# One of the seven products of a gate/up stage done by a second level of Strassen's form, for two feature tiles at a time

## The chip, the cores and the metric

The kernel runs on one core of a Trainium2 chip. The time is device time in microseconds (us). The core has an engine for matmuls (PE, with its weight loads shown apart as PEld), a vector engine (DVE), a scalar engine (ACT), GpSimd (POOL) and SyncE (SP), which here issues nearly all DMAs. Each engine takes its instructions in the order of the program and waits on semaphores for the others.

## The reference, cut to what matters

The program is one step of a hybrid decoder layer on 1048 tokens (16 meta tokens, 1024 of a prompt, 8 samples) of width 1024: a feed-forward block, a mixing stage (HGRN2 and Mamba-2 heads with their projections), a second feed-forward block and a final norm. The change is in the two feed-forward blocks (FFN), each with 2816 hidden features:

```python
def swiglu(x, wg, wu, wd):
    return (jax.nn.silu(x @ wg) * (x @ wu)) @ wd

h = h + 0.5 * swiglu(rmsnorm(h, n1), w1g, w1u, w1d)
...
h = h + 0.5 * swiglu(rmsnorm(h, n2), w2g, w2u, w2d)
```

All is in float32. The second FFN leaves out the 16 meta tokens and has 1032.

## The kernel before, in words

**Precision.** A float32 product is made of three matmuls with operands split into a high and a low part (`mm3`, L160 to L165): high x high, high x low, low x high. The high part of a weight is a cast on ACT, the low part a subtraction on DVE (`Left.hi` L460 and `Left.lo` L464, the records of L462 and L466).

**Gate and up as one Strassen product.** A feature tile is 128 of the 2816 hidden features; there are 22 in each FFN, taken in eleven pairs. For one tile, the left side is a 2 x 2 block matrix: gate and up weights by the two halves of the 1024 input features. The right side is the input, in two halves of the features and two lanes of the tokens. Seven products (Strassen's form with few additions) give gate and up for both lanes: `g0`, `g1`, `u0`, `u1`. Tokens are in four quarters of Q (262 in the first FFN, 258 in the second); a product is made for two halves of the tokens, `c` = 0 and 1, and each of these is four blocks of 128 input features x three matmuls of Q columns: 12 matmuls, one step. A tile has 14 steps in the order of `ORDER` = 1, 6, 2, 5, 7, 3, 4. The operands of the seven products (`Blocks`, L317) lie in SBUF for the whole stage, in 28 of the 30 buffers "u".

**Weights.** `Left` loads the four blocks of a tile (products 1, 7, 4, 2), forms the four others by sums on DVE (L458) and splits all seven. `plan` (L472) says ahead of which step each is issued, counted from the tile's first step: loads at -11 and -10, sums at -7 to -5, the cast of the i-th product at 2i - 4 and its subtraction at 2i - 3. Raw blocks have eight buffers "r", split ones six buffers "ws".

**After a product.** Products 2, 3 and 4 accumulate into the banks of 1, 5 and 7. There are two buffers of two PSUM banks, taken in turns, and four single banks "mis", which this stage uses in its first tile alone. `post` (L549) runs behind the second half's step: after 1 a copy on ACT (L551), after 6, 5, 7, 3 and 4 an addition on DVE (L553, L560, L562, L564, L572), after 2 a multiplication by the norm's factor (`times_r`, L546) and silu on ACT (L558). After 3 follow the factor for `g1` and `u1` and silu (L581), after 4 the factor for `u0` and both hidden products (`product_`, L587).

**Hidden blocks.** `Hidden.jobs` (L629) forms, for each pair of tiles, four differences of hidden blocks on DVE (L647) for the down projection, itself in Strassen's form, and stores all seven operands to DRAM (L650) through SP. They are issued ahead of given steps of the second tile and of the next pair.

**The order** is written out by hand: `Steps` (L416) holds PE's steps, and ahead of each step the functions registered for it; `ffn` (around L810 to L832) fixes the order of PE, DVE, ACT and SP to that of the program. `down` begins where the last pair ends; its loads and splits (L667, L671, L675, L717, L732, L737) are registered for steps before that. In the first FFN, the first tile's rows are late and finished in the second pair's first steps.

Of the kernel before, what the change touches and what calls it, by code (L numbers as in the profile page):

```python
# [9 lines left out]
F32 = mybir.dt.float32  # L10
F32R = mybir.dt.float32r
# [6 lines left out]
P = 128  # L18
# [298 lines left out]
class Blocks:  # L317
# [123 lines left out]
class Left:  # L441
# [80 lines left out]
def halves(t):  # L522
    return t.rearrange("p (c t) -> p c t", c=2)


def pair(K, S, wg, wu, f, ops, spread, hid, late_r, first=None):
# [16 lines left out]

    def times_r(n, i, cs, src=None):
        t = temp(n, cs)
        nc.vector.tensor_mul(t, t if src is None else src, spread.lanes(i, cs))  # L546
        return t

    def post(p, cs, b):  # L549
        if p == 1:  # L550
            nc.scalar.copy(temp("z", cs), b)  # L551
        elif p == 6:
            nc.vector.tensor_add(temp("v", cs), b, temp("z", cs))  # L553
        elif p == 2 and (f == 0 or wait and f == 1):
            nc.scalar.copy(temp("g0", cs), b)
        elif p == 2:
            t = times_r("g0", 0, cs, b)
            nc.scalar.activation(t, t, AF.Silu)  # L558
        elif p == 5:
            nc.vector.tensor_add(temp("x", cs), b, temp("v", cs))  # L560
        elif p == 7:
            nc.vector.tensor_add(temp("u1", cs), b, temp("x", cs))  # L562
        elif p == 3:
            nc.vector.tensor_add(temp("g1", cs), b, temp("v", cs))  # L564
# [5 lines left out]
            times_r("u1", 1, cs)  # L570
        else:
            nc.vector.tensor_add(temp("u0", cs), b, temp("v", cs))  # L572
            if f == 0:
                return
            times_r("u0", 0, cs)
            for n in range(2):
                product_(n, cs)

    def silu(n, cs):
        t = times_r(f"g{n}", n, cs)  # L580
        nc.scalar.activation(t, t, AF.Silu)  # L581

    def product_(n, cs):
        if "h" not in tm:
            tm["h"] = True
            hid.append(K.slot("s", K.T))
        nc.vector.tensor_mul(halves(hid[0][:, n * 2 * K.Q : n * 2 * K.Q + 2 * K.Q])[:, cs], temp(f"g{n}", cs), temp(f"u{n}", cs))  # L587

    if not first:
# [32 lines left out]
class Hidden:  # L622
# [6 lines left out]
    def jobs(self, S, i, hid, e0, e1):  # L629

        K = self.K
        t, b = {}, {}

        def block(n):

            return hid[n // 2][0][:, n % 2 * 2 * self.K.Q : n % 2 * 2 * self.K.Q + 2 * self.K.Q]

        def val(p):
            return b[p] if p in b else block({1: 0, 12: 1, 2: 2, 3: 3}[p])

        def sub(p, x, y):
            s = {5: 0, 6: 0, 7: 1, 4: 1}[p]
            if s not in t:
                t[s] = K.slot("s", self.K.T)
            o = (p in (6, 4)) * 2 * self.K.Q
            b[p] = t[s][:, o : o + 2 * self.K.Q]
            K.nc.vector.tensor_sub(b[p], val(x), val(y))  # L647

        def store(p):
            K.nc.sync.dma_start(self.d[p][:, :, i, :], halves(val(p)))  # L650
# [5 lines left out]
        for at, p in ((e0 + 2, 1), (e1 + 1, 3), (e1 + 2, 2)):  # L656
            S.before(at, lambda p=p: store(p))

    def load(self, S, p, at):
# [147 lines left out]
def ffn(K, wg, wu, wd, ops, spread, src, first, after, late_r):  # L807

    NF = DFF // P
    wgv = wg.rearrange("(k p) c -> p k c", p=P)
    wuv = wu.rearrange("(k p) c -> p k c", p=P)
    wdv = wd.rearrange("(f p) c -> p f c", p=P)
    E = mybir.EngineType

    with K.tc.manual_schedule(engines={E.PE, E.DVE, E.Activation, E.SP}):
        S = Steps()
        S.before(14, lambda: K.banks(2))
        hidden = Hidden(K)  # L820
        for i in range(NF // 2):
            hid, e = [], []
            for f in (2 * i, 2 * i + 1):
                hid.append([])
                pair(K, S, wgv, wuv, f, ops, spread, hid[-1], late_r, first if f == 0 else None)
                e.append(len(S.steps))
            hidden.jobs(S, i, hid, *([late_r + 6, max(late_r + 7, e[1])] if i == 0 else e))
        h = []
        down(K, S, wdv, hidden, src, h, after)
        S.run()  # L830
    return h
# [1252 lines left out]
```

## Time and profile before

| | us |
|---|---|
| median of three runs | 1995.35 |
| lowest and highest of them | 1993.51, 1996.27 |
| span of the profiled execution, first to last instruction | 1985.6 |
| busy in it: PE, its weight loads | 1935.3, 1897.1 |
| busy in it: DVE, ACT, POOL | 1452.2, 834.8, 82.3 |

The profiled execution is one more execution; the page gives its span and no time around it. Busy times overlap, as the engines run beside each other. The gate/up stage of the first FFN ends near 490 us of the span, that of the second runs from about 1300 to 1741 us. In rows of the order of time the columns are: start, duration, engine, line, operation, output <- input, shape, and in brackets how long the engine stood idle before and what ended that.

### The profile page before, as it was taken

The page shows a single profiled execution, that of the slowest core. Times are in us where ns is not written, and L with a number is a line of the kernel's source. Part 1 is how long each engine was busy: PE and PEld are TensorE (multiplying, and loading weights), DVE is VectorE, ACT ScalarE, POOL GpSimd, SP SyncE. Part 2 cuts the span into 40 slices and gives each one's busy share as a digit, 9 for nine tenths or more (in the row PEclk, how much of TensorE's full clock was granted, in tenths as well). Part 3 has the DMA queues.
Part 4 walks back from the last instruction along what each step waited for, and adds up shares of the span by engine and source line. Part 5 has one row for each costly group of instructions (what it writes and reads, how often), then busy time and mean ns, then how long its engine had stood idle before and what let it go on. Part 6 is the DMA issues. An engine that isn't in the chain of part 4 may idle for free.

```text
span 1985.6 us, 40881 instructions
## 1 busy us (share of the span) xinstructions
PE 1935.3 (97%) x16681; PEld 1897.1 (96%) x16681; DVE 1452.2 (73%) x2504; ACT 834.8 (42%) x1591; POOL 82.3 (4%) x135
## 2 busy tenths in 40 slices
PE   7999999999999999999999999999999999999997
PEld 6999999999999999998988989999999999999997
DVE  7777777777688776676655547887777777768973
ACT  7522222224534655465544535742222222344352
POOL 4000000000000310000000001200000000000000
PEclk9999999999999999999999999999999999999999
DMA  6233242324976542222522154224232433587851
GB/s 218 77 100 98 82 129 82 111 83 155 299 242 222 181 126 60 65 91 75 168 78 76 57 168 135 74 81 128 81 112 81 118 92 103 157 243 238 273 178 69
DMA packets 323876, 258.45 MB, mean 130 GB/s; under 512 B 17568, under 2 KB 299424, under 8 KB 323680
## 3 DMA queue, kind: packets, MB, share of 16 engines
q1 hardware_dynamic: 323448, 255.79, 42.0%
q8 instruction: 132, 2.16, 0.4%
q14 instruction: 56, 0.46, 0.1%
q0 software_dynamic: 224, 0.04, 0.0%
q10 hardware_dynamic: 16, 0.00, 0.0%
HBM read 190.79 MB, written 65.05 MB: 129 GB/s over the span
## 4 chain that ended last, share of the span: by engine, by line
PE 77%; DVE 12%; DMA 4%; ACT 4%; issue 2%; SPq 1%; POOL 0%; DVEq 0%; ACTq 0%; POOLq 0%
PE acc L163 24%; PE acc L165 24%; PE acc L164 23%; DVE u L675 1%; DVE u L352 1%; DVE ws L737 1%; DMA r<-in_w_ffn_up_dram 1%; DVE s L761 1%; DMA s<-in_x_prompt_dram 1%; DVE ws L466 1%; DVE u L727 1%; DMA r<-in_w_ffn_down_dram 1%; DMA u<-hd 1%; DVE t L546 1%; ACT ws L732 1%
## 5 line engine op out<-in xcount | busy, mean ns | idle before, releaser
L163 PE MATMUL acc<-u,ws 128*128 128x258 f32 (+4 forms) x4504 | 1314.6, 292 | 8.9 <-DVE t L562 1.9
L165 PE MATMUL acc<-u,ws 128*128 128x258 f32 (+4 forms) x4504 | 1304.8, 290 | 3.5 <-DVE ws L466 3.4
L164 PE MATMUL acc<-u,ws 128*128 128x258 f32 (+4 forms) x4504 | 1304.9, 290 | 3.2 <-DVE u L352 2.6
L163 PEld LDWEIGHTS acc<-u,ws 128*128 128x128 f32 x4504 | 852.3, 189 | 14.8 <-issue 5.3
L164 PEld LDWEIGHTS acc<-u,ws 128*128 128x128 f32 x4504 | 855.5, 190 | 6.2 <-DVE u L352 3.8
L165 PEld LDWEIGHTS acc<-u,ws 128*128 128x128 f32 x4504 | 852.0, 189 | 5.1 <-DVE ws L466 4.6
L466 DVE TENSOR_TENSOR ws<-r,ws 128x512 fp32r<-128x512 f32 x308 | 212.6, 691 | 78.9 <-ACT ws L462 78.9
L462 ACT CAST ws<-r 128x512 fp32r<-128x512 f32 x308 | 173.8, 614 | 5.2 <-DVE r L458 4.6
L581 ACT ACTIVATE t<-t 128x524 f32<-128x524 f32 (+1 forms) x47 | 29.9, 640 | 298.3 <-DVE t L546 298.3
L458 DVE TENSOR_TENSOR r<-r,r 128x512 f32<-128x512 f32 x176 | 121.1, 690 | 9.7 <-DMA r<-in_w_ffn_up_dram 8.0
L558 ACT ACTIVATE t<-t 128x516 f32<-128x516 f32 (+1 forms) x41 | 26.2, 639 | 201.5 <-DVE t L546 201.5
L675 DVE TENSOR_TENSOR u<-u,u 128x1048 fp32r<-128x1048 f32 (+3 forms) x84 | 97.1, 1158 | 10.2 <-ACT u L671 10.2
L546 DVE TENSOR_TENSOR t<-t,u 128x524 f32<-128x524 f32 (+1 forms) x135 | 90.3, 697 | 2.8
L230 POOL TENSOR_TENSOR t<-t,t 128x262 f32<-128x262 f32 (+1 forms) x56 | 54.4, 980 | 830.6 <-ACT t L229 827.4
L158 DVE TENSOR_TENSOR ws<-r,ws 128x512 fp32r<-128x512 f32 x88 | 60.6, 699 | 34.9 <-ACT ws L157 34.5
L732 ACT CAST ws<-u 128x512 fp32r<-128x512 f32 (+1 forms) x72 | 42.2, 586 | 99.8 <-DVE u L727 97.8
L671 ACT CAST u<-u 128x1048 fp32r<-128x1048 f32 (+3 forms) x84 | 82.8, 988 | 1.3 <-DMA u<-hd 1.3
L761 DVE SCALAR_TENSOR_TENSOR s<-acc,s 128x524 f32<-128x524 f32 (+3 forms) x88 | 54.6, 644 | 36.4 <-PE acc L165 36.1
L737 DVE TENSOR_TENSOR ws<-r,ws 128x512 fp32r<-128x512 f32 (+1 forms) x84 | 57.3, 693 | 29.2 <-ACT ws L732 29.2
L732 ACT CAST ws<-r 128x512 fp32r<-128x512 f32 (+1 forms) x84 | 47.5, 582 | 65.2 <-DVE r L727 34.8
L551 ACT COPY t<-acc 128x524 f32<-128x524 f32 (+3 forms) x46 | 26.4, 574 | 103.6 <-PE acc L165 103.6
L157 ACT CAST ws<-r 128x512 fp32r<-128x512 f32 x88 | 53.7, 618 | 32.4 <-PE acc L165 28.5
(386 smaller groups left out, 1833.3 us busy)
## 6 DMA issues: line engine op xcount, KB each, us to landing
r<-in_w_ffn_down_dram SPq DMA_DIRECT2D x128, 256.0 KB
hd<-s SPq DMA_DIRECT2D x93, 258.0 KB
r<-in_w_ffn_gate_dram SPq DMA_DIRECT2D x88, 256.0 KB
r<-in_w_ffn_up_dram SPq DMA_DIRECT2D x88, 256.0 KB
hd<-s SPq DMA_DIRECT2D x77, 262.0 KB
u<-hd SPq DMA_DIRECT2D x36, 516.0 KB
u<-hd SPq DMA_DIRECT2D x28, 524.0 KB
r<-in_w_in_dram SPq DMA_DIRECT2D x56, 256.0 KB
```

Of the source, the lines that this page charges most:

```text
L163: mm(ps, whi, xhi, start=first, stop=False, skip_group_check=more)
L164: mm(ps, whi, xlo, start=False, stop=False, skip_group_check=more)
L165: mm(ps, wlo, xhi, start=False, stop=last, skip_group_check=more)
L458: self.K.nc.vector.tensor_tensor(self.raw[p], self.raw[x], self.raw[y], op)
L462: self.K.nc.scalar.copy(self.w[p][:, : self.n * P], self.raw[p])
L466: self.K.nc.vector.tensor_sub(t[:, 512 : 512 + w], self.raw[p], t[:, :w].bitcast(F32))
L546: nc.vector.tensor_mul(t, t if src is None else src, spread.lanes(i, cs))
L671: K.nc.scalar.copy(hi, lo.bitcast(F32))
L675: K.nc.vector.tensor_sub(lo, lo.bitcast(F32), hi.bitcast(F32))
L732: nc.scalar.copy(w[p, j, g][:, : n * P], src)
L737: nc.vector.tensor_sub(t[:, 512 : 512 + n * P], box[0], t[:, : n * P].bitcast(F32))
L761: nc.vector.scalar_tensor_tensor(t, b, 0.5, t, ALU.mult, ALU.add)
```

## The change

From the third pair of each FFN (the fifth tile) on, a tile makes six of its seven products itself, in the order `ORDER6`. Product 3 of both tiles of the pair is made together: the left side is a 2 x 2 block matrix (two tiles by two halves of the product's 512 input features), the right side the operand of product 3 (the same halves by the two token halves `c`), and seven inner products of two blocks each take the place of two times two halves of four blocks. An inner product is 2 x 3 = 6 matmuls of Q columns. A pair now has 12 steps for tile A, and for tile B ten, two inner ones (products 1 and 6; 5 and 7), the two of product 4, and two inner ones (2 and 3; 4), the last with 6 matmuls. The inner products go into the four "mis" banks.

Their results are added, Q columns at a time, to what the tile holds as `x` (the sums after product 5), so `x` becomes `g1`; what the second tile's bank after 4 gives goes into `v`, which becomes `u0`. The gate multiplication and silu for `g1` and the hidden product of lane 1 of both tiles come after the last inner step, at the next pair's first four steps, and the differences and their stores later than before. The raw weights of product 3 are kept unsplit until tile B, where four sums, four casts and four subtractions make the inner left operands. The right operands (three new ones, one written in place) are made once in each FFN, during the second pair and the first tile of the third.

```diff
-    def plan(self, S, s0, late, sums):
+    def plan(self, S, s0, late, sums, order=ORDER, last=0):
+        n = len(order)
+        his = [2 * i - 4 + late + last * (i == n - 1) for i in range(n)]
...
-            (ORDER, [2 * i - 4 + late for i in range(7)], self.hi),
-            (ORDER, [2 * i - 3 + late for i in range(7)], self.lo),
+            (order, his, self.hi),
+            (order, [d + 1 for d in his], self.lo),
...
+ORDER6 = (1, 6, 2, 5, 7, 4)
+class Inner:
+    def operands(self):
...
+        return [
+            lambda: whole(a, 1, 0), lambda: whole(b, 0, 0), lambda: sub(b, a, b), lambda: cast(5, b), lambda: low(5, b),
+            lambda: whole(d, 1, 1), lambda: sub(b, d, b), lambda: cast(6, b), lambda: low(6, b),
+            lambda: sub(a, d, a), lambda: cast(7, a), lambda: low(7, a),
+            lambda: whole(d, 0, 1), lambda: sub(b, d, b),
+        ], [lambda: cast(4, b), lambda: low(4, b)]
...
+        for at, fn, *args in (
+            (2, sums), (3, sum7), (5, hi, 0, f), (6, lo, 0, f), (6, sum3), (6, hi, 1, s), (7, lo, 1, s),
+            (7, hi, 2, g), (8, lo, 2, g), (9, hi, 3, f[:, 256:]), (10, lo, 3, f[:, 256:]),
+        ):
+            S.before(s0 + at, lambda fn=fn, args=args: fn(*args))
...
+    def product(self, p):
...
+        for k in range(2):
+            wh, wl = (w[:, x + k * P : x + k * P + P] for x in (o, 512 + o))
+            ks = slice(k * K.Q, k * K.Q + K.Q)
+            K.mm3(self.ps[b], wh, wl, hi[:, ks], lo[:, ks], new and k == 0, k == 1, not new)
+    def post(self, p):
...
+        if p == 1:
+            nc.scalar.copy(z, ps)
+        elif p == 6:
+            add(v, ps, z)
+            add(y, y, v[:, None, :].broadcast_to([P, 2, self.K.Q]))
+            add(x[:, 1], x[:, 1], v)
+        elif p == 5:
+            add(y[:, 1], ps, y[:, 1])
+        else:
+            t = {7: y[:, 1], 2: x[:, 0], 3: x[:, 1], 4: y[:, 0]}[p]
+            add(t, ps, t)
...
+        if i == 0:
+            both(*ORDER6)
+            return
+        S.before(s0 + 1, lambda: inner.begin(S, s0))
+        both(1, 6, 2, 5, 7)
+        inner.step(S, 1, 6)
+        inner.step(S, 5, 7)
+        both(4)
+        inner.step(S, 2, 3)
+        inner.step(S, 4)
+        e = len(S.steps)
+        for at, fn in enumerate((inner.then[0][0], inner.then[1][0], inner.then[0][1], inner.then[1][1])):
+            S.before(e + at, fn)
...
-        ks = (1, 3, 5) if i < FP - 1 else (1, 2, 3)
-        for at, args in zip((e0 + 1, *(e1 + k for k in ks)), ((5, 12, 1), (6, 3, 5), (7, 3, 12), (4, 2, 6))):
+        ats = (e0 + 1, e1 + 1, e1 + 3, e1 + 5) if not inner else (e1 + 4, e1 + 5, e1 + 7, e1 + 9) if i < FP - 1 else (e1 + 4, e1 + 5, e1 + 6, e1 + 7)
+        for at, args in zip(ats, ((5, 12, 1), (6, 3, 5), (7, 3, 12), (4, 2, 6))):
...
+            rec = inner.next() if i >= 2 else None
+            if i == 1:
+                def operands(s0=len(S.steps)):
+                    made, late = inner.operands()
+                    for n, fn in enumerate(made):
+                        S.before(s0 + 5 + 2 * n + n // 4, fn)
+                    for n, fn in enumerate(late):
+                        S.before(s0 + 36 + 2 * n, fn)
```

More of the change, by code (lines that the diff above doesn't have):

```diff
@@ L532, in pair @@
+def pair(K, S, wg, wu, f, ops, spread, hid, late_r, first=None, inner=None):
     nc = K.nc
@@ L562, in post @@
             nc.vector.tensor_add(temp("u1", cs), b, temp("x", cs))
+            if inner:
+                times_r("u1", 1, cs)
         elif p == 3:
@@ L570, in post @@
             times_r("u1", 1, cs)
+        elif inner:
+            t = temp("v", cs)
+            nc.vector.tensor_add(t, b, t)
+            tm["u0"] = tm["v"]
+            times_r("u0", 0, cs)
+            product_(0, cs)
         else:
@@ L587, in product_, with both, keep, gate @@
         nc.vector.tensor_mul(halves(hid[0][:, n * 2 * K.Q : n * 2 * K.Q + 2 * K.Q])[:, cs], temp(f"g{n}", cs), temp(f"u{n}", cs))
+    if inner:
+        i = f % 2
+        left.plan(S, s0, 0, 0, ORDER6, 2 * i)
+        unit = Unit(K, left.w, [o.op for o in ops], 4, post)
+        def both(*ps):
+            for p in ps:
+                for c in range(2):
+                    unit.step(S, p, c, (0, 1))
+        def keep():
+            inner.raw[i] = left.raw[3]
+        cs = slice(0, 2)
+        def gate():
+            tm["g1"] = tm["x"]
+            silu(1, cs)
+        S.before(s0 - 4, keep)
+        inner.then[i] = (gate, lambda: product_(1, cs))
+        inner.out[i] = lambda: temp("x", cs)
+        if i == 0:
[11 more added lines that the diff above has]
+            S.before(e + at, fn)
+        return
     if not first:
@@ L627, in __init__, with jobs @@
         self.d = {p: K.dram.tile([P, 2, FP, self.K.Q], F32, name=K.uid("hd")) for p in ORDER}
-    def jobs(self, S, i, hid, e0, e1):
+    def jobs(self, S, i, hid, e0, e1, inner):
         K = self.K
@@ L650, in store @@
             K.nc.sync.dma_start(self.d[p][:, :, i, :], halves(val(p)))
-        ks = (1, 3, 5) if i < FP - 1 else (1, 2, 3)
-        for at, args in zip((e0 + 1, *(e1 + k for k in ks)), ((5, 12, 1), (6, 3, 5), (7, 3, 12), (4, 2, 6))):
+        ats = (e0 + 1, e1 + 1, e1 + 3, e1 + 5) if not inner else (e1 + 4, e1 + 5, e1 + 7, e1 + 9) if i < FP - 1 else (e1 + 4, e1 + 5, e1 + 6, e1 + 7)
+        for at, args in zip(ats, ((5, 12, 1), (6, 3, 5), (7, 3, 12), (4, 2, 6))):
             S.before(at, lambda args=args: sub(*args))
             S.before(at + 2, lambda p=args[0]: store(p))
-        for at, p in ((e0 + 2, 1), (e1 + 1, 3), (e1 + 2, 2)):
+        for at, p in ((e0 + 2, 1), (e1 + (5 if inner else 1), 3), (e1 + 2, 2)):
             S.before(at, lambda p=p: store(p))
@@ L820, in ffn @@
         hidden = Hidden(K)
+        inner = Inner(K, ops)
         for i in range(NF // 2):
             hid, e = [], []
+            rec = inner.next() if i >= 2 else None
[6 more added lines that the diff above has]
+                        S.before(s0 + 36 + 2 * n, fn)
+                S.before(len(S.steps) + 4, operands)
             for f in (2 * i, 2 * i + 1):
                 hid.append([])
-                pair(K, S, wgv, wuv, f, ops, spread, hid[-1], late_r, first if f == 0 else None)
+                pair(K, S, wgv, wuv, f, ops, spread, hid[-1], late_r, first if f == 0 else None, rec)
                 e.append(len(S.steps))
-            hidden.jobs(S, i, hid, *([late_r + 6, max(late_r + 7, e[1])] if i == 0 else e))
+            hidden.jobs(S, i, hid, *([late_r + 6, max(late_r + 7, e[1])] if i == 0 else e), rec)
         h = []
```

63 lines of the change are left out of this document (62 added, 1 removed).

## The prediction

> **What bounds the kernel now.** I read the page's busy shares first, then a table of stretches, then the order of time on DVE inside one gate/up stage, and last who PE waited for.
>
> ```profile
> span 1985.6 us, 40881 instructions
> PE 1935.3 (97%) x16681; PEld 1897.1 (96%) x16681; DVE 1452.2 (73%) x2504; ACT 834.8 (42%) x1591; POOL 82.3 (4%) x135
> ...
> 300.00:400.00 100.00, 100.00 (x824) 100.00 (x823) 74.75 (x117) 27.52 (x50) 0.00 (x0) 1.00 0.33 97
> 1600.00:1700.00 100.00, 99.86 (x833) 99.68 (x833) 75.22 (x119) 27.42 (x50) 0.00 (x0) 1.00 0.33 96
> ```
>
> The last two rows give, for a stretch in the first and in the second FFN's gate/up stage, the busy time of PE, its weight loads, DVE, ACT and POOL, then the granted clock, the DMA share and GB/s. PE has no gap, the clock is whole, DVE has a quarter free and DMA two thirds. So in this stage the time is the number of matmuls times what one takes; the rest matters where it makes PE wait. What one matmul takes, from DVE rows that waited for PE:
>
> ```profile
> 220.52 0.70 DVE L564 TENSOR_TENSOR t<-acc,t 128x524 f32<-128x524 f32 x1 [0.73 <-PE acc L165]
> ...
> 261.44 0.70 DVE L564 TENSOR_TENSOR t<-acc,t 128x524 f32<-128x524 f32 x1 [0.67 <-PE acc L165]
> 262.18 1.32 DVE L546 TENSOR_TENSOR t<-t,u 128x524 f32<-128x524 f32 x2
> ...
> 1333.40 0.69 DVE L564 TENSOR_TENSOR t<-acc,t 128x516 f32<-128x516 f32 x1 [0.98 <-PE acc L165]
> ...
> 1373.66 0.69 DVE L564 TENSOR_TENSOR t<-acc,t 128x516 f32<-128x516 f32 x1 [1.09 <-PE acc L165]
> ```
>
> L564 is the step after product 3, once a feature tile. Two tiles (336 matmuls) lie between the rows: 40.92 us in the first FFN, 40.26 in the second, so 0.1218 and 0.1198 us a matmul. One step of 12 takes 1.461 and 1.438 us.
>
> **The change part by part.** *Matmuls.* Of each pair from the third on, product 3 of two tiles (2 tiles x 2 token halves x 4 blocks x 3 = 48) becomes seven products of 2 blocks x 3: 42. Six fewer in each of nine pairs, in two FFNs: 54 x 0.1218 = 6.58 and 54 x 0.1198 = 6.47, together **13.05 us less**. The order of the built program has the same 108 matmuls fewer. I take the rate of before for the new ones, which go in groups of six into other banks; groups into those banks are in the trace:
>
> ```profile
> L163 PE MATMUL acc<-u,ws 128*128 128x258 f32 (+4 forms) x4504 | 1314.6, 292 | 8.9 <-DVE t L562 1.9
> ...
> L163 PE MATMUL mis<-u,ws 128*128 128x262 f32 (+1 forms) x32 | 9.4, 294 | 0.1
> ```
>
> The mean is 294 ns against 292, and nothing waited in front. The two ends: no extra cost, or those 2 ns on 42 x 18 matmuls, 1.5 us; I take none, since matmuls overlap.
>
> The Trainium skill, TensorE: Matmul & The Clock Gate, section "Wait — 56ns, not 53.3ns?", puts a warm matmul at N/2.4 + 2.5 ns; by it 262 and 258 columns would be 111.7 and 110.0 ns and the saving an estimated 12.0 us. The rows above say 121.8 and 119.8, and they decide.
>
> *DVE and ACT, per pair.* Gone: two splits of product 3's weights on each engine (L466, L462) and two steps after it (L564). New on DVE: four 256-wide sums, three 512-wide and one 256-wide split, seven 262-wide steps and one 524-wide with a repeated operand. So 48 wide operations stay 48, and 12 quarter ones are added. What they cost from start to start:
>
> ```profile
> 27.67 0.43 DVE L553 TENSOR_TENSOR t<-acc,t 128x262 f32<-128x262 f32 x1 [0.37 <-PE acc L165]
> 28.13 0.43 DVE L560 TENSOR_TENSOR t<-acc,t 128x262 f32<-128x262 f32 x1
> 28.48 1.24 DVE L352 TENSOR_TENSOR u<-u,u 128x1048 fp32r<-128x1048 f32 x1
> ...
> 236.70 0.68 DVE L458 TENSOR_TENSOR r<-r,r 128x512 f32<-128x512 f32 x1
> 237.30 0.69 DVE L466 TENSOR_TENSOR ws<-r,ws 128x512 fp32r<-128x512 f32 x1
> 237.90 0.69 DVE L458 TENSOR_TENSOR r<-r,r 128x512 f32<-128x512 f32 x1
> ```
>
> A wide one holds the next back 0.61 us, 0.73 where the next reads its result (261.44 to 262.18 above); a 262-wide one 0.35 (28.13 to 28.48), 0.46 where it is read (27.67 to 28.13). Per pair: before 48 x 0.61 + 15 x 0.12 = 31 of 40.9 us, the 75% of the windows; after, 12 x 0.34 more, **35.2 of 40.2 us, 88%**. ACT, at 27%, gets some 1.4 us more. The repeated operand has no row: between 0.61 (its width) and 1.16 (the 1048-wide rows' spacing); I take 0.61.
>
> *Does DVE stay ahead?* Room in the sum isn't enough: DVE works in order, and PE waits if DVE reads a bank or writes weights too late. I follow DVE through the seam of two pairs, first FFN, us from the pair's first matmul. Tile A has 12 steps, tile B 15.5, so the next pair starts at 40.19. DVE waits for product 5 of B (eight steps into B) and starts at 29.43. From there to the last inner step stand 15 wide and 8 quarter operations with 6 dependences: 9.15 + 2.72 + 0.72 = 12.6, to 42.0, 1.8 us into the next pair. On the way it has read the bank of inner product 5 by 37.5 (inner 3 goes into it at 38.7), that of inner 7 by 37.8 (inner 4 at 39.5), and written the next tile's second weights by 41.8 (used at 43.1). Then come two gate multiplies, and a wait for ACT, whose silu stands ahead of a cast:
>
> ```profile
> 242.46 0.64 ACT L581 ACTIVATE t<-t 128x524 f32<-128x524 f32 x1 [7.29 <-DVE t L546]
> 243.00 1.13 ACT L462 CAST ws<-r 128x512 fp32r<-128x512 f32 x2
> ```
>
> Silu 0.54 and cast 0.57 after the first multiply: DVE goes on at 44.0 with four wide ones (to 46.4), the step after product 6, two differences, a split and two sums (3.9), and at 50.3 takes product 2's bank, read out at 51.0. Product 7 wants that bank eight steps into the pair, at 51.9. **The least margin is 0.9 us**; by the end of tile A DVE waits for PE again. So no wait of PE per pair.
>
> *SP and the buffers.* The differences of a pair's hidden blocks and their stores move some four steps later, to steps 4 to 11 of the next tile A, since the second token halves are ready only after the gates. SP takes its queue in order, and weight loads stand behind stores:
>
> ```profile
> SPq L650 <- DVE s L587: 581.5, 42, 16.3
> ...
> 250.48 1.07 SPq L452 DMA_DIRECT2D r<-in_w_ffn_up_dram  x2
> ...
> 255.73 1.42 DVE L458 TENSOR_TENSOR r<-r,r 128x512 f32<-128x512 f32 x2 [0.42 <-DMA r<-in_w_ffn_up_dram]
> ```
>
> From the issue of two loads to the sums that waited for them are 5.25 us. In the new order tile B's loads (steps 1 and 2 of A) have only the store of a block made in step 13 of the B before ahead of them, and the next A's (steps 5 and 6 of B) the stores of differences that DVE made by step 9 of A. Keeping two raw pieces longer leaves all eight raw buffers in use: tile B's second "up" load waits for the split that DVE ends at 41.8, so it is there by 47.6 and summed at 49; the last load waits for the split that ends at 44.6 and is there by 50.4, used at 52. Nothing late, by 1.4 us. The inner operands keep three of the eight "s" buffers; hidden blocks and differences need four at once, so they fit.
>
> *The start.* In the second pair DVE makes the inner operands, 12 wide operations two steps apart (ACT: 4 casts). Three fall where product 3 and 4 still wait for DVE's reads:
>
> ```profile
> 93.50 0.69 DVE L560 TENSOR_TENSOR t<-acc,t 128x524 f32<-128x524 f32 x1
> ...
> 96.53 0.69 DVE L562 TENSOR_TENSOR t<-acc,t 128x524 f32<-128x524 f32 x1
> ...
> 106.53 0.70 DVE L553 TENSOR_TENSOR t<-acc,t 128x524 f32<-128x524 f32 x1 [0.32 <-PE acc L165]
> ...
> 1342.03 0.70 DVE L553 TENSOR_TENSOR t<-acc,t 128x516 f32<-128x516 f32 x1
> ...
> 1344.90 0.69 DVE L546 TENSOR_TENSOR t<-acc,u 128x516 f32<-128x516 f32 x1 [0.97 <-PE acc L165]
> ...
> 1349.25 0.69 DVE L560 TENSOR_TENSOR t<-acc,t 128x516 f32<-128x516 f32 x1
> ...
> 1351.66 0.69 DVE L562 TENSOR_TENSOR t<-acc,t 128x516 f32<-128x516 f32 x1
> ```
>
> 106.53 waited for PE four steps into tile 3 (0.2 us after the last matmul), so tile 2 began at 80.03 and its product 3 at 94.64; product 5's bank was read by 94.19, a margin of 0.45. Two operations ahead (1.22) make it 0.77 late; a third with its dependence (0.73) makes product 7's bank 99.17 against 98.33: 0.84 more. First FFN: 1.6 us. In the second the first operation fits into the 0.97 of idle time, the second meets a margin of 0.52 (read 1349.94, product 3 at 1350.46), the third one of 1.0: together 0.35. **2.0 us more.** If the idle time is no cover there, 1.6 as well, so 3.2.
>
> *The end of the stage* costs something already:
>
> ```profile
> PE acc L163 <- DVE t L562: 0.9, 1, 0.9
> ...
> PE acc L163 <- DVE t L562: 1.0, 1, 1.0
> PE acc L163 <- DVE t L560: 0.3, 1, 0.3
> ...
> 480.65 1.25 DVE L675 TENSOR_TENSOR u<-u,u 128x1048 fp32r<-128x1048 f32 x1 [0.28 <-ACT u L671]
> 481.81 0.68 DVE L737 TENSOR_TENSOR ws<-r,ws 128x512 fp32r<-128x512 f32 x1
> ```
>
> These are PE's waits around the last tile, first FFN at 455 to 520 us, then the second at 1700 to 1800: 2.2 us, since DVE also splits the hidden blocks for down (1.16 each). In the new order those stand between the inner steps; ACT's copy after inner 1 stands behind a cast whose weight buffer is free only when inner 5 is through. Followed as above from the last tile's product 5, that copy is done at 18.0 us of the tile, inner 5's bank is read at 21.9, and inner 3 wanted it at 21.2: 0.75 us a FFN. Products 3 and 4 no longer wait there. So 1.5 in place of 2.2: **0.7 less**. DVE is then some 6 us behind when down begins; its pieces for down's first products come at 28.4 and 29.0 against uses at 30.3 and 31.4.
>
> *Sum:* -13.05 + 2.0 - 0.7 = **-11.8 us**, from the profiled execution's span of 1985.6 to 1973.8. The page gives no time around that span; the median of the runs shown, 1995.35, lies 9.75 above it, and I leave that as it is: **1983.6 us**.
>
> **The rivals.** *DVE gives half of it back.* The margin of 0.9 rests on about 36 operations; 0.035 us more for each and PE waits some 0.35 us a pair: 18 x 0.35 = 6.3, so 1989.9. For it speaks the 88%; against it that the spacings are read from the same lines in the same stage.
>
> *Slower: each operation at the seam holds DVE for its whole duration.* Then 24 independent ones between 29.4 and 51.0 cost 0.69 or 0.43 in place of 0.61 or 0.35, 1.9 us more; less the margin, PE waits 1.05 us in each of 18 pairs, 18.9 us: 1995.35 - 11.8 + 18.9 = 2002.5. It decides from 0.65 us a pair on, where the 11.8 are gone: 0.043 us more per operation. Against it: 236.70, 237.30, 237.90 above, where each row starts before the one ahead has ended.
>
> The Trainium skill, VectorE: DVE Perf Modes, section "The DRAIN you can't avoid", says that the next operation does not start until the pipe of the one before is empty, and to keep the number of operations down; read as whole durations, that is this rival. The rows disagree by 0.08 us an operation; what they can't show is an inner step on a 262-wide strided half.
>
> *The edges cost more.* If the second pair and the two ends cost 3 us more (3.2 for the start, and 2 more where down begins, with 6 us of lag), 1986.8.
>
> *It doesn't do what it says:* the matmul count says it does; only inner matmuls slower than the others would be that case, and 0.1218 would have to become 0.137 in the 756 new ones to undo the 11.8.
>
> **How the numbers follow.** Forecast 0.58; edges dearer 0.12; half given back 0.18; slower 0.10; 0.02 for the last. About 0.2% (4 us) is what a measurement here tells from no change. Half given back is by 5.5 us under the median in the middle; so I put 0.12 of its 0.18 within 4 us and 0.06 beyond, and the last case within. Faster 0.58 + 0.12 + 0.06 = 0.76, same 0.12 + 0.02 = 0.14, slower 0.10. Range: downward, no cost at the start or the ends (15.3 less, 1980.0); upward through the half case to 1994.0, beyond which lie the slower case and the worst of the half, under 0.2.
>
> **What would show it.** 108 matmuls fewer; 40.2 us from pair to pair in the first FFN and 39.5 in the second; DVE near 87% there and some 105 us busier in all; no PE wait on the step after product 2 in the third to tenth pairs; a wait of about 1 us in the second pair, and one on inner 5's bank of 0.75 in the last. Wrong it is if PE waits in every pair for the multiply after product 2 or for the next tile's splits, or if the inner groups run slower than 0.122 us a matmul.

## The result and the profile after

The changed kernel takes **2015.62 us** (median of 4 runs, 2013.87 to 2017.68), the kernel before, run beside it, 1994.91 (1993.51 to 1996.27): ratio 1.0105, 95% interval 1.0091 to 1.0119, so 20.7 us slower. The forecast was 11.8 us faster.

The page of the kernel after: span, busy shares, and the costliest PE group (behind the second bar its idle time and what ended most of it).

```profile
span 2016.0 us, 40978 instructions
...
PE 1939.5 (96%) x16573; PEld 1898.7 (94%) x16573; DVE 1543.0 (77%) x2744; ACT 860.3 (43%) x1653; POOL 85.0 (4%) x135
...
L163 PE MATMUL acc<-u,ws 128*128 128x258 f32 (+4 forms) x4216 | 1239.6, 294 | 38.1 <-DVE t L686 24.3
```

The 108 matmuls are gone (16681 to 16573) and DVE is 90.8 us busier, where some 105 were reckoned. New is idle time: L163, the first matmul of each group of three, waited 38.1 us where it was 8.9, and 24.3 of it for DVE's L686, the step after product 7. The table of stretches, same columns as before:

```profile
300.00:400.00 100.00, 96.14 (x786) 95.59 (x785) 84.78 (x144) 27.86 (x53) 0.00 (x0) 1.00 0.31 97
...
1600.00:1700.00 100.00, 96.95 (x808) 96.59 (x807) 86.49 (x150) 29.68 (x57) 0.00 (x0) 1.00 0.34 101
```

PE, which had no gap, now stands 3 to 4 us in 100; DVE is at 85 and 86%, not full. Whom PE waited for, kernel after, at 60 to 520 us and then at 1300 to 1800 (total, times, longest):

```profile
PE acc L163 <- DVE t L686: 11.2, 9, 1.3
PE acc L163 <- DVE t L670: 2.5, 1, 2.5
PE acc L163 <- DVE t L684: 2.2, 2, 1.5
PE mis L163 <- DVE t L644: 0.6, 1, 0.6
...
PE acc L163 <- DVE t L686: 13.1, 9, 1.5
PE acc L163 <- DVE t L670: 2.4, 1, 2.4
...
PE mis L163 <- DVE t L644: 0.7, 1, 0.7
```

Nine waits for L686 in each FFN: one a pair from the third on. The third pair's is 0.89 us, each of the others some 1.29 in the first FFN and 1.52 in the second. How long a pair takes is read from ACT's copy after product 1 of tile B, which starts as soon as PE ends that product:

```profile
191.86 0.60 ACT L675 COPY t<-acc 128x524 f32<-128x524 f32 x1 [8.65 <-PE acc L165]
...
233.58 0.60 ACT L675 COPY t<-acc 128x524 f32<-128x524 f32 x1 [8.60 <-PE acc L165]
...
1461.28 0.59 ACT L675 COPY t<-acc 128x516 f32<-128x516 f32 x1 [8.50 <-PE acc L165]
...
1502.57 0.59 ACT L675 COPY t<-acc 128x516 f32<-128x516 f32 x1 [8.49 <-PE acc L165]
```

41.72 us in the first FFN and 41.29 in the second, against 40.92 and 40.26 before and 40.19 and 39.53 that 330 matmuls take: 1.53 and 1.76 us of each steady pair is stall.

**Where it stalls.** PE and then DVE at the end of one tile A, kernel after, in order of time:

```profile
309.39 0.28 PE L165 MATMUL acc<-u,ws 128*128 128x262 f32 x1
310.96 0.36 PE L163 MATMUL acc<-u,ws 128*128 128x262 f32 x1 [1.29 <-DVE t L686]
```

```profile
308.29 0.70 DVE L684 TENSOR_TENSOR t<-acc,t 128x524 f32<-128x524 f32 x1
308.90 0.69 DVE L816 TENSOR_TENSOR s<-s,s 128x524 f32<-128x524 f32 x1
309.52 0.68 DVE L466 TENSOR_TENSOR ws<-r,ws 128x512 fp32r<-128x512 f32 x1
310.12 0.70 DVE L686 TENSOR_TENSOR t<-acc,t 128x524 f32<-128x524 f32 x1
```

The matmul at 309.39 is the last of product 7, the one at 310.96 the first of product 4. Product 4 accumulates into the bank of product 7, so it can't begin before DVE (310.12 to 310.82) has read it. Before the change product 3 (24 matmuls, 2.9 us) lay between the two. The change takes 3 out of tile A's order and leaves 7 and 4 side by side; in tile B two inner steps stand there. DVE was also late: PE's last result was there at 309.67, and DVE began 0.45 later, busy with a difference and a split.

**Tile 4**, the first with twelve steps, costs more: from its copy after product 1 (127.16 in the first FFN, 1397.46 in the second) to that of tile 5 are 22.92 and 22.52 us; its matmuls take 17.53 and 17.26. SP, DVE and PE of the kernel after, in order:

```profile
128.12 0.52 SPq L819 DMA_DIRECT2D hd<-s  x1
128.73 0.88 SPq L452 DMA_DIRECT2D r<-in_w_ffn_gate_dram  x1
...
130.85 0.60 SPq L452 DMA_DIRECT2D r<-in_w_ffn_up_dram  x1
```

```profile
126.77 1.32 DVE L719 TENSOR_TENSOR s<-t,t 128x524 f32<-128x524 f32 x2
...
136.24 1.42 DVE L458 TENSOR_TENSOR r<-r,r 128x512 f32<-128x512 f32 x2 [2.53 <-DMA r<-in_w_ffn_up_dram]
```

```profile
138.42 0.36 PE L163 MATMUL acc<-u,ws 128*128 128x262 f32 x1 [2.50 <-DVE t L670]
...
139.38 0.42 PE L163 MATMUL acc<-u,ws 128*128 128x262 f32 x1
139.60 0.42 PE L164 MATMUL acc<-u,ws 128*128 128x262 f32 x1
...
142.43 0.28 PE L165 MATMUL acc<-u,ws 128*128 128x262 f32 x1
142.55 0.29 PE L163 MATMUL acc<-u,ws 128*128 128x262 f32 x1
```

SP's store of a hidden block waits for DVE's product (126.77 to 128.09); tile 5's weight loads stand behind it; DVE's sums wait 2.53 us for the loads; the step after product 2 stands behind the sums, and PE waits 2.50 us for that. Then some 16 matmuls come 0.22 us apart where it is 0.12 otherwise, 1.5 us more.

### The profile page after: what moved, and what is told of

Its sections match the earlier page's. It is cut to its first block, busy times and chain, and to the rows that moved or that the text cites. A ratio compares the mean times of both kernels' runs of the same rounds, so it can differ in the third digit from the quotient of the medians.

```text
span 2016.0 us, 40978 instructions
## 1 busy us (share of the span) xinstructions
PE 1939.5 (96%) x16573; PEld 1898.7 (94%) x16573; DVE 1543.0 (77%) x2744; ACT 860.3 (43%) x1653; POOL 85.0 (4%) x135
## 4 chain that ended last, share of the span: by engine, by line
PE 52%; DVE 33%; issue 5%; DMA 5%; ACT 4%; SPq 0%; POOL 0%; DVEq 0%; ACTq 0%; POOLq 0%
PE acc L163 15%; PE acc L165 15%; PE acc L164 15%; DVE r L458 5%; DVE ws L466 4%; DVE t L670 2%; DVE u L844 2%; DVE s L719 2%; DMA r<-in_w_ffn_down_dram 2%; DVE ws L906 1%; DVE u L896 1%; DVE s L930 1%; DVE t L647 1%; DVE s L816 1%; DVE t L686 1%
## 5 line engine op out<-in xcount | busy, mean ns | idle before, releaser
L163 PE MATMUL acc<-u,ws 128*128 128x258 f32 (+4 forms) x4216 | 1239.6, 294 | 38.1 <-DVE t L686 24.3
L164 PE MATMUL acc<-u,ws 128*128 128x258 f32 (+4 forms) x4216 | 1227.8, 291 | 3.8 <-DVE u L352 2.0
L165 PE MATMUL acc<-u,ws 128*128 128x258 f32 (+4 forms) x4216 | 1227.2, 291 | 2.7 <-DVE ws L466 2.6
L163 PEld LDWEIGHTS acc<-u,ws 128*128 128x128 f32 x4216 | 802.8, 190 | 48.8 <-issue 38.9
L164 PEld LDWEIGHTS acc<-u,ws 128*128 128x128 f32 x4216 | 804.9, 191 | 6.4 <-DVE u L352 2.7
L165 PEld LDWEIGHTS acc<-u,ws 128*128 128x128 f32 x4216 | 802.1, 190 | 4.3 <-DVE ws L466 3.9
L466 DVE TENSOR_TENSOR ws<-r,ws 128x512 fp32r<-128x512 f32 x272 | 188.1, 692 | 32.9 <-ACT ws L462 32.8
L462 ACT CAST ws<-r 128x512 fp32r<-128x512 f32 x272 | 157.3, 617 | 15.1 <-ACT ws L462 9.9
L670 DVE TENSOR_TENSOR t<-t,u 128x524 f32<-128x524 f32 (+1 forms) x135 | 91.8, 697 | 2.8
L158 DVE TENSOR_TENSOR ws<-r,ws 128x512 fp32r<-128x512 f32 x88 | 60.1, 693 | 35.3 <-ACT ws L157 34.8
L157 ACT CAST ws<-r 128x512 fp32r<-128x512 f32 x88 | 53.7, 617 | 33.2 <-PE acc L165 29.0
```

The lines of the kernel that those rows point to most:

```text
L163: mm(ps, whi, xhi, start=first, stop=False, skip_group_check=more)
L164: mm(ps, whi, xlo, start=False, stop=False, skip_group_check=more)
L165: mm(ps, wlo, xhi, start=False, stop=last, skip_group_check=more)
L462: self.K.nc.scalar.copy(self.w[p][:, : self.n * P], self.raw[p])
L466: self.K.nc.vector.tensor_sub(t[:, 512 : 512 + w], self.raw[p], t[:, :w].bitcast(F32))
```

## The experiments

Two theories of the repeated wait. **Bank:** product 4 comes right behind the product whose bank it needs, so PE stands for one read of DVE, however free DVE is. **Load:** DVE, at 85%, is behind there, and would be wherever PE needs it next.

**a1_swap4: product 4 of tile A behind product 1 of tile B**

```diff
-            both(*ORDER6)
+            both(*ORDER6[:-1])
+            inner.four = lambda: both(4)
...
-        both(1, 6, 2, 5, 7)
+        both(1)
+        inner.four()
+        both(6, 2, 5, 7)
```

(The split of tile B's first weights is two steps earlier with it, the store of one hidden block four later.)

> The changed kernel with two products changing places: product 4 of tile A comes behind product 1 of tile B, so that a product lies between 7 and 4, which share a bank. The same instructions on every engine. Bank theory (product 4 of tile A goes into the bank of product 7, which is the product right ahead of it, so PE stands while DVE wakes up and reads that bank, however free DVE is): the waits on the step after product 7, 11.2 and 13.1 us in the two FFNs, go, from tile B to tile B it is 40.2 us in the first FFN (41.74 in the changed kernel) and 39.5 in the second (41.29): 18 pairs by about 1.65 us, about 1986 us. Load theory (DVE, 85% busy, is behind at that point, and would be behind wherever PE needs it next): the waits turn up at another step and the time stays between 2005 and 2016.

Measured: 2009.04 us, ratio 1.008 (1.0049 to 1.0111). PE's waits in this kernel, first and second FFN:

```profile
PE acc L163 <- DVE t L699: 8.0, 9, 0.9
...
PE acc L163 <- DVE t L699: 7.9, 9, 0.9
```

The waits for L686 are gone and as many for L699, the step after product 4, have come. By the time alone load has it. But the built order shows why: there are two buffers of two banks; while tile B's product 1 holds one, its product 6 takes the other, which product 4 has just filled. I had made the same neighbourhood again. One of these places, DVE and then PE:

```profile
230.83 0.70 DVE L699 TENSOR_TENSOR t<-acc,t 128x524 f32<-128x524 f32 x1 [1.07 <-PE acc L165]
```

```profile
231.68 0.36 PE L163 MATMUL acc<-u,ws 128*128 128x262 f32 x1 [0.89 <-DVE t L699]
```

DVE had stood idle for 1.07 us and began the read 0.04 us after PE's last result, and PE waited 0.89 us all the same. So the time doesn't decide, but this wait can't be DVE being behind; b1 below is the mended form.

**a2_split7: the step after product 7 by halves**

```diff
+            both(*ORDER6[:-2])
+            for c in range(2):
+                S.add(mm, lambda c=c: post(7, slice(c, c + 1), unit.bank(7, (0, 1), False)[:, c : c + 1]))
+            both(4)
```

(mm is the 12 matmuls of that half.)

> The changed kernel in its own order, but the step after product 7 of tile A is done for each token half behind that half's matmuls: the first half's read lies beside the second half's 1.46 us of matmuls, and product 4's first half then waits for the first half's read alone. DVE gets one 262-wide operation more for each pair (0.35 us). Bank theory: no wait over 0.2 us ahead of product 4, 18 pairs by about 1.5 us less, 1986 to 1991 us. Load theory: DVE has more to do, so the waits stay or grow: 2015 or more.

Measured: 2034.14 us, ratio 1.0211 (1.0182 to 1.024). That is load's range (2015 or more), but both expectations miss why. PE in the first FFN:

```profile
314.38 0.39 PE L163 MATMUL acc<-u,ws 128*128 128x262 f32 x1 [1.36 <-DVE t L686]
...
316.73 0.36 PE L163 MATMUL acc<-u,ws 128*128 128x262 f32 x1 [0.61 <-DVE t L686]
```

There are two waits a pair now, 18 in each FFN. Twelve matmuls lie between these rows: the first wait is that of product 7's own second half for the read of its first half, in another bank of the same buffer. In the built program the wait is for the buffer, not the bank, so halving the read made two waits of one: 37.8 us of them in the two FFNs together, against 24.3 in the changed kernel.

**a3_order_in_before: the same neighbourhood in the kernel before**

```diff
+        o = (1, 6, 2, 5, 7, 4, 3) if f > 3 and f % 2 == 0 else ORDER
```

> The kernel before, no inner products, with product 4 right behind product 7 (order 1, 6, 2, 5, 7, 4, 3) in the first tile of each pair from the third on, and the steps after 4 and 3 exchanged to fit; the same number of matmuls and of DVE operations. DVE is 75% busy in it. Bank theory: one stall of at least 1.2 us (wake-up 0.2, read 0.7, back to PE 0.15, refill) and about 1.45 in each of 18 pairs: 22 to 27 us more than the kernel before, 2017 to 2022. Load theory: with a quarter of DVE free nothing is lost: 1993 to 1998.

Measured: 2025.79 us, ratio 1.0172 (1.014 to 1.0204), 32 us over the kernel before.

```profile
PE acc L163 <- DVE t L562: 15.3, 10, 2.1
...
PE acc L163 <- DVE t L562: 16.6, 10, 2.4
```

These waits, first and second FFN, are for L562, that kernel's step after product 7. It has no inner products and a DVE with a quarter free, and loses 1.8 us at each of 18 places: the neighbourhood makes the stall without them. It is more than the 1.45 expected, as DVE, though a quarter free over the stage, was busy with other operations just there and began the 18 reads 0.5 to 1.6 us after PE's last result.

**c2_moved: two differences out of DVE's way**

```diff
-        ... else (e1 + 4, e1 + 5, e1 + 7, e1 + 9) if i < FP - 1 else ...
+        ... else (e1 + 4, e1 + 5, e1 + 10, e1 + 11) if i < FP - 1 else ...
```

> The same two differences moved in the changed kernel itself, its order of products kept. There DVE starts the read of product 7's bank 0.25 us (first FFN) and about 0.5 us (second) later than PE's last matmul allows, being busy with these differences and splits; the read and the way back take the rest of the 1.53 and 1.76 us lost in a pair. Bank theory: 0.25 and 0.5 us less in 8 pairs each, 1.25 us stay: about 6 us less than the changed kernel, 2007 to 2012. Load theory (DVE's load makes the whole stall): 8 pairs each at 40.2 and 39.5 us, 24 us less, about 1991.

Measured: 2005.34 us, ratio 1.0064 (1.0045 to 1.0083). Tile B's copies after product 1:

```profile
189.91 0.60 ACT L675 COPY t<-acc 128x524 f32<-128x524 f32 x1 [8.25 <-PE acc L165]
...
231.23 0.60 ACT L675 COPY t<-acc 128x524 f32<-128x524 f32 x1 [8.20 <-PE acc L165]
```

41.32 us a pair; in the second FFN 40.67 (1454.48 to 1495.15). Over the matmuls that is 1.13 and 1.14 us: with DVE out of the way (it begins these reads 0.03 to 0.06 us after PE's last result) the stall is the same in both FFNs, and that is the price of the neighbourhood. The other 0.40 and 0.62 us of 1.53 and 1.76 were DVE being late, somewhat more than the 0.25 and 0.5 expected; so the time lies 2 us under the bank theory's range, and 14 over the load theory's 1991.

**b1_swap_order: no product behind one with its bank**

As a1, and:

```diff
-        both(6, 2, 5, 7)
+        both(2, 6, 5, 7)
```

> As a1_swap4 (product 4 of tile A behind product 1 of tile B), and product 2 of tile B ahead of its product 6. In a1 the wait went from the step after product 7 to the step after product 4 (8.0 and 7.9 us in the two FFNs): with two buffers, product 6 of tile B took the bank that product 4 had just filled. In this order no product goes into the bank of the one right ahead of it: 7 A, 1 B, 4 A, 2 B, 6 B, 5 B alternate. Bank theory: no wait in a steady pair, 40.2 us a pair in the first FFN (changed kernel 41.74) and 39.5 in the second (41.29), 27 to 30 us less than the changed kernel, 1986 to 1989. Load theory (DVE, 85% busy, is late wherever PE needs it): a third place for the wait, and 2003 to 2012 as a1 had.

Measured: 1989.58 us, 26.0 under the changed kernel (the kernel before took 1992.41 beside this one and 1994.91 beside the changed kernel), ratio to before 0.9981 (0.9966 to 0.9996). The nine waits of each FFN behind product 7 are gone, with the same instructions on DVE. That is the bank theory's time within 1 us. A pair takes 40.47 us (186.30 to 226.77) and 40.04 (1441.45 to 1481.49), so 0.28 and 0.51 stay; the waits of the second FFN name them:

```profile
PE acc L163 <- DVE t L684: 3.3, 9, 1.0
```

**b2_loads_first: the stores behind the loads, in the changed kernel**

```diff
-        for at, p in ((e0 + 2, 1), (e1 + (5 if inner else 1), 3), (e1 + 2, 2)):
+        for at, p in ((e0 + 2, 1), (e1 + (5 if inner else 3 if i == 1 else 1), 3), (e1 + (3 if i == 1 else 2), 2)):
```

> The changed kernel with two stores of the second pair's hidden blocks moved two steps and one step later, behind tile 5's weight loads in SP's queue; nothing else. In the changed kernel tile 4 (the first of 12 steps) took 3.9 us in the first FFN and 3.5 in the second more than its matmuls and its stall behind product 7; DVE stood there 2.5 and 2.9 us for the up weights, loaded behind a store that waited for DVE's last hidden product, while the sums that need them come two steps earlier in a tile of 12 steps. Queue theory: the loads leave before tile 4 begins, that wait goes: 7 us less, 2006 to 2010. Theory that it is DVE's own lag from making the operands: no difference, 2014 to 2017.

Measured: 2006.87 us, 8.8 under the changed kernel, ratio 1.0065 (1.0048 to 1.0083). From tile 4's copy to tile 5's:

```profile
126.46 0.60 ACT L675 COPY t<-acc 128x524 f32<-128x524 f32 x1 [1.50 <-PE acc L165]
...
145.67 0.60 ACT L675 COPY t<-acc 128x524 f32<-128x524 f32 x1 [7.50 <-PE acc L165]
```

19.21 us where it was 22.92, and in the second FFN 18.52 (1392.71 to 1411.23) where it was 22.52: 7.7 us together, with PE's wait for L670 gone in both. The queue theory stands. In the sum of tile 4 it was 2.5 us of wait, the slow matmuls behind it, and little else.

**a4_no_operands: the inner operands not made**

```diff
-                S.before(len(S.steps) + 4, operands)
+                S.before(len(S.steps) + 4, lambda: inner.op.update({p: inner.half(p % 2, p // 2 % 2) for p in range(1, 8)}))
```

> The changed kernel without the 14 operations that make the inner products' right operands in the second pair (10 sums and lows on DVE, 4 casts on ACT, and the two late ones): the inner products read parts of product 3's operand as it is, so part of the computation is left out. From the traces the start of the change takes about 7.5 us in the first FFN and 3.8 in the second more than the matmuls give (post-1 copies of tiles 3, 4 and 5 against those of the kernel before). Theory that these operations delay DVE, and through the hidden blocks the stores and the weight loads behind them in SP's queue, and through the loads DVE again: about 11 us less than the changed kernel, 2004. The prediction's own reckoning (only the few operations that lie ahead of products 3 and 4): 2 us less, 2013.6.

Measured: 2011.57 us, ratio 1.0096 (1.007 to 1.0121), 4 us under the changed kernel, between the two expectations; the intervals of the two ratios overlap, so the time doesn't decide. The profile parts them. In the first FFN tiles 2 and 3 take 21.54 and 20.46 us again, as in the kernel before (tile 3's copy at 102.86, tile 4's at 123.32), where the changed kernel lost 1.8 in each (104.90, 127.16): 3.6 us are the operands. In the second FFN nothing changes (tile 4 22.62 us). How DVE's delay grew there, SP of the changed kernel, then of this one:

```profile
85.90 22.23 SPq L819 DMA_DIRECT2D hd<-s  x9
```

```profile
85.66 19.79 SPq L819 DMA_DIRECT2D hd<-s  x9
```

Nine stores, most of them waiting for DVE, take 2.4 us longer, and tile 4's loads stand behind them; in the changed kernel DVE then waits 2.46 us for these loads (at 115.84) and PE 1.46 us for DVE (at 118.02). Without the operands none of this shows. Tile 4 of the first FFN, too, takes 20.88 us (123.32 to 144.20) in place of 22.92: 2.0 us of its loss come from the same delay. The rest of the 11 us expected is the queue's at tile 4, which b2 has.

**b3_all: b1, b2, and the operands begun five steps later**

```diff
-                        S.before(s0 + 5 + 2 * n + n // 4, fn)
+                        S.before(s0 + 10 + 2 * n, fn)
...
-                        S.before(s0 + 36 + 2 * n, fn)
+                        S.before(s0 + 40 + 2 * n, fn)
```

> b1 and b2 together, and the making of the operands begun five steps later (at step 10 of the second pair), away from the late work on the first tile, which cost 3.6 us in the first FFN (a4_no_operands has tiles 2 and 3 at the pace of the kernel before). If the three losses are separate, they add: 28 by the order, 7 by the loads, 2 by the later start: about 1978 us, 15 below the kernel before. If they hide each other (a stall gives DVE time to catch up, and without it the next limit shows, DVE at 88% above all): 1985 to 1995.

Measured: 1982.44 us, ratio 0.9943 (0.9924 to 0.9962); again as **d2_b3_again** 1983.24, 0.9944 (0.9927 to 0.9961).

> b3_all again, beside d1_split_later on the same chip: ratio to the kernel before 0.9924 to 0.9962 as in its first call, steady pairs of 40.42 and 40.07 us.

The losses add, short by some 4 us: a pair still takes 40.42 and 40.07 us. PE of this kernel in the second FFN, at product 1 of tile B:

```profile
1591.21 0.36 PE L163 MATMUL acc<-u,ws 128*128 128x258 f32 x1 [0.28 <-DVE t L684]
```

DVE reads product 5's bank too late, at the end of 30 us (from 1603.6 of one pair to 1633.6) with a single pause of 0.6.

**c1_all_moved: b3 with c2's edit**

> b3_all with two of the four differences of hidden blocks in each pair done later, behind the step after product 7 of tile A (where DVE then stands idle), their stores with them. In b3_all a steady pair still takes 40.42 us in the first FFN and 40.07 in the second, 0.24 and 0.54 over its matmuls: DVE works without a pause from 1603.6 to 1633.6 us and reads product 5's bank 0.28 us too late for product 1 of tile B. Theory that this is the rest of DVE's load at the seam: 0.2 and 0.5 us less a pair, about 6 us less than b3_all, 1976. Rival (a cost of the order itself, DVE's place in it does not matter): 1980 to 1985, as b3_all.

Measured: 1982.92 us, ratio 0.9951 (0.9933 to 0.9969): no gain, the first theory falls. (The time is the rival's, a cost of the order itself; but d1 below keeps the order and has no gap.) DVE and then ACT in the same place:

```profile
1589.96 0.69 DVE L670 TENSOR_TENSOR t<-acc,u 128x516 f32<-128x516 f32 x1
...
1591.86 0.69 DVE L466 TENSOR_TENSOR ws<-r,ws 128x512 fp32r<-128x512 f32 x1 [0.61 <-ACT ws L462]
```

```profile
1590.68 0.64 ACT L682 ACTIVATE t<-t 128x516 f32<-128x516 f32 x1 [5.00 <-DVE t L670]
1591.23 1.65 ACT L462 CAST ws<-r 128x512 fp32r<-128x512 f32 x3
```

The 0.6 us of work taken out became 0.61 us of waiting. DVE's step after product 2 releases ACT's silu; the casts stand behind the silu; DVE's split waits for the cast; and the read of product 5's bank stands behind the splits. It is a chain through two engines, not a sum of work.

**d1_split_later: one split and one sum out of that chain**

```diff
-        left.plan(S, s0, 0, 0, (1, 2, 6, 5, 7, 4) if i else ORDER6, 2 * i, i)
+        left.plan(S, s0, 0, 0, (1, 2, 6, 5, 7, 4) if i else ORDER6, 2, i)
...
-            ((5, 6, 7, 3), [d + sums for d in (-7, -7, -6, -5)], self.sum_),
+            ((5, 6, 7, 3), [d + sums for d in (-7, -7, -6, -5 + 2 * early)], self.sum_),
```

> b3_all with the cast and split of product 4's weights of tile A two steps later, and with it tile B's last sum (its raw weights come into the buffer that the split frees). In c1_all_moved two differences fewer stood ahead of the step after product 5, and the wait of PE stayed at 0.29 us: DVE stood 0.61 us for a cast that ACT does behind the silu of g0, and then did two splits, for products 4 of A and 1 of B, one after the other. Theory that this chain (step after product 2, silu, two casts, two splits, step after product 5) sets the 0.24 and 0.54 us a pair: with one cast, one split and one sum fewer in it the wait goes, 40.2 and 39.55 us a pair, 6 us less than b3_all in the same call. Rival (DVE's load in the whole seam): a wait of the same size at another step, no difference.

Measured: **1976.86 us, ratio 0.9912 (0.9891 to 0.9934)**, 6.4 us under b3_all as run beside it (d2_b3_again) and 16.9 under the kernel before. The stretches and tile B's copies of this kernel:

```profile
300.00:400.00 100.00, 100.00 (x824) 100.00 (x823) 85.13 (x148) 31.21 (x59) 0.00 (x0) 1.00 0.31 94
1600.00:1700.00 100.00, 100.00 (x836) 100.00 (x836) 89.29 (x157) 29.53 (x56) 0.00 (x0) 1.00 0.34 101
```

```profile
180.49 0.60 ACT L675 COPY t<-acc 128x524 f32<-128x524 f32 x1 [4.12 <-PE acc L165]
...
220.67 0.60 ACT L675 COPY t<-acc 128x524 f32<-128x524 f32 x1 [4.68 <-PE acc L165]
...
1430.46 0.59 ACT L675 COPY t<-acc 128x516 f32<-128x516 f32 x1 [3.96 <-PE acc L165]
...
1469.98 0.59 ACT L675 COPY t<-acc 128x516 f32<-128x516 f32 x1 [4.40 <-PE acc L165]
```

PE has no gap in either stretch, with DVE at 85 and 89%. A pair takes 40.18 and 39.52 us; 330 matmuls were reckoned at 40.19 and 39.53.

**c0_before: the kernel before once more**

> The kernel before once more, for a second profile of it: its first profiled execution has a span of 1985.6 us, 8 us under the fastest of the three times shown, while the changed kernel's span lies 1.7 us under its own time. If a span is always about 1.7 us under the time, this one is at 1988 to 1996, and the difference to the first profile lies in stretches that the change does not touch; tile to tile in gate and up stays 20.46 and 20.12 us.

Measured: 1988.14 us with a span of 1986.3, 1.8 under it; tiles keep their pace. In every execution profiled with its time known the span lies 1.7 to 1.9 us under that time. So the execution first profiled took an estimated 1987 us, at the low end of what this kernel takes (1986.28 to 1999.99 in the runs here); the 9.75 us that the prediction left as time around the span are mostly the spread of executions.

## Why the prediction was wrong, by its own steps

| part, us, both FFNs | forecast | measured |
|---|---|---|
| 108 matmuls fewer | -13.05 | held: pairs in d1 at the reckoned pace |
| stall in each pair | 0 | +28.6 (8 x 1.53, 8 x 1.76, and 1.13 for the shorter first wait of each FFN, as in c2) |
| tile 4 and its loads | 0 | +8.4 (22.92 - 17.53 - 1.13 and 22.52 - 17.26 - 1.13) |
| operands in the second pair | +2.0 | +3.6 |
| end of the stage | -0.7 | near it: waits of 0.6 and 0.7 on inner product 5's bank, 0.75 forecast |

The last column sums to +26.8 with -0.7 for the end; the profiled spans differ by 30.4, the medians by 20.7. Most of the 3.6 us between sum and spans lies outside the change. From the first record of the mixing stage's projection to the first copy of the second FFN, before and after, columns as in the stretches:

```profile
716.73:1293.99 577.26, 561.93 (x5429) 533.13 (x5428) 380.69 (x838) 312.02 (x642) 34.17 (x57) 0.99 0.31 94
...
731.59:1311.98 580.39, 566.68 (x5429) 537.94 (x5427) 380.32 (x838) 312.01 (x642) 34.68 (x57) 0.98 0.32 94
```

The same matmuls and the same operations of DVE and ACT take 3.1 us longer there, at a granted clock of 0.98 for 0.99. The medians' 20.7 is 6 us less than the sum: the spans compare a low execution of before with the highest of after, and none of the kernel before near its median was profiled, so where the 6 us lie stays open.

**The step that failed is "So no wait of PE per pair."** It rests on a walk through the seam from tile B's product 5 to the next tile A's product 7, and stops there with "by the end of tile A DVE waits for PE again". That DVE waits for PE was taken as the end of danger. But where DVE waits for the very product that PE's next one needs, PE waits in turn. The order was in the prediction's own text (product 4 into the bank of 7), and the count of twelve steps for tile A had taken product 3 out; the order of banks wasn't gone through again. a3 shows that this neighbourhood costs the kernel before 32 us with no inner product in it, b1 that another order removes this stall with as many instructions on every engine, and c2 that its price is 1.13 us where DVE is free.

The Trainium skill, Perfetto Trace Analysis, section "Matmuls", says that independent groups of matmuls should rotate through PSUM banks, so that the reading of one lies beside the next group. The traces agree: no wait where buffers alternate (d1), 1.13 us where they don't (c2). It would have named this step.

**"Nothing late, by 1.4 us"** (SP and the buffers) was reckoned for the steady pair and not for the first: there the second pair's stores still stand ahead of the loads, and a tile of twelve steps needs its sums two steps sooner. It cost 7.7 us by b2. One of the prediction's own signs showed here, though in one pair only: PE waited for the step after product 2, 2.50 and 2.39 us.

**The start** was priced by the operations ahead of products 3 and 4 alone. That DVE's lag goes through the stores to the loads and back to DVE (22.23 against 19.79 us of SP) was left out: 3.6 for 1.6 in the first FFN; in the second 0.35 was forecast and none is seen.

**The rivals.** The slower one had the sign and, with 1.05 us a pair, not far from the size, but for a reason that the trace denies: DVE's rows still start 0.61 us apart (308.29, 308.90, 309.52 above). "Half given back" is there beneath the stall: 0.28 and 0.51 us a pair in b1, 0.35 forecast; but it was a chain with ACT's silu and casts, and d1 ends it with as many operations on DVE (2744). 88% was no bound.

## What to carry to other kernels

When a step is taken out of an order, write down which buffer each remaining step fills and who must have read it, and look at every new pair of neighbours, not only at the place where work was added. A margin of an in-order engine is the longest chain up to a given read, through other engines too; its busy share says little. Queues must be followed in the first and the last round apart from the steady one.

## What the runs showed of the hardware

A wait of PE can cost more than its length. Behind the waits of 2.50 us (138.42) and 2.39 us (1408.43) of the changed kernel some 16 matmuls of 262 or 258 columns came about 0.22 us apart, over some 3.4 us, with a granted clock of 0.86 at 134 to 146 us; behind its 18 waits for product 7's bank, of at most 1.5 us, none did. In a3 a wait of 2.39 us was followed by the same, and in b1 one of 1.80 (at 1393.84, with a granted clock of 0.86 at 1390 to 1402 us), while two of 2.09 and 2.18 in a3 were not, so the length alone doesn't decide. The Trainium skill, TensorE: Matmul & The Clock Gate, section "What's actually happening", says that the array gets 1.2 GHz in place of 2.4 after an idle window of some 3.4 us, and that these windows run freely: 262 columns at 1.2 GHz are an estimated 0.218 us, which the rows 139.38 and 139.60 show. The same page of the Trainium skill, section "HAM oscillation — how this bites in real kernels", puts the danger at gaps over 3.4 us; here 1.80 were enough.
